# Cutting the last two rows of a row-sum kernel into other pieces: row 7 in five instead of four, row 6 in two instead of three

## The chip, the cores and the metric

One core of one Trainium2 chip. The time is the device time of one execution, in microseconds (us). DVE is VectorE, ACT is ScalarE, SP the engine that issues most transfers (SPq in the profile).

## The reference

```python
# x, y: float32, 1024 rows of 4096 columns; axis = -1
def reference(x, y, axis):
    return np.sum(np.abs(x - y), axis=axis).astype(np.float32)
```

33.55 MB are read, 4 KB are written, and each element needs a subtraction, an absolute value and an addition.

## The kernel before

Each of the 128 partitions holds eight rows, called row 0 to row 7 here. Rows 0 to 3 of x and of y are loaded by one transfer each. Then x rows 4 to 6 follow in one transfer, and their y rows one by one, each as soon as a buffer of y is free. Row 7 comes in pieces, x and y of each piece by a transfer of their own. DVE subtracts; ACT takes the absolute value and sums along the row in the same instruction, and a read of its accumulator (186 to 188 ns in the profile of before) follows each. The last piece of row 7 doesn't go through ACT. DVE writes its difference beside the sums that ACT left of the other pieces and closes with one reduction over both, with absolute values.

```python
PIECES = [1984, 1088, 640, 384]      # row 7
ROW6 = [2048, 1024, 1024]            # row 6
# ... transfers of rows 0 to 6 cut
    o = 0
    for i, w in enumerate(PIECES):
        c = slice(o, o + w)
        put(lambda: nc.sync.dma_start(out=xb[:, H - 1, c], in_=xr[:, K - 1, c]).then_inc(s_piece[i], 16))
        if i == 0:
            put(lambda: nc.sync.wait_ge(s_sub, H))
        put(lambda: nc.sync.dma_start(out=yb[:, H - 1, c], in_=yr[:, K - 1, c]).then_inc(s_piece[i], 16))
        o += w

    def sub(tx, ty, waits):          # DVE
        for s, v in waits:
            put(lambda: nc.vector.wait_ge(s, v))
        put(lambda: nc.vector.tensor_sub(out=tx, in0=tx, in1=ty).then_inc(s_sub, 1))
        count[0] += 1

    def absum(tx, to, sem):          # ACT
        put(lambda: nc.scalar.wait_ge(s_sub, count[0]))
        put(lambda: nc.scalar.activation(tx, tx, ABS, accum_out=to).then_inc(sem, 1))
        count[1] += sem is s_act
# ... rows 0 to 3 cut
    for k in range(H - 2):           # rows 4 and 5, whole
        sub(xb[:, k, :], yb[:, k, :], ([(s_xb, 16)] if k == 0 else []) + [(s_row[k], 16)])
        absum(xb[:, k, :], ro[:, H + k:H + k + 1], s_act)
    o = 0
    for i, w in enumerate(ROW6):     # row 6
        c = slice(o, o + w)
        sub(xb[:, H - 2, c], yb[:, H - 2, c], [(s_row[H - 2], 16)] if i == 0 else [])
        absum(xb[:, H - 2, c], part6[:, i:i + 1], s_act)
        o += w
    done6 = count[1]
    o = 0
    for i, w in enumerate(PIECES):   # row 7
        c = slice(o, o + w)
        tx, ty = xb[:, H - 1, c], yb[:, H - 1, c]
        if i == 1:                   # the sums of row 6's parts
            put(lambda: nc.vector.wait_ge(s_act, done6))
            put(lambda: nc.vector.reduce_sum(out=ro[:, K - 2:K - 1], in_=part6, axis=AX).then_inc(s_end, 1))
        if i < n_part:
            sub(tx, ty, [(s_piece[i], 32)])
            absum(tx, last[:, i:i + 1], s_end)
        else:
            put(lambda: nc.vector.wait_ge(s_piece[i], 32))
            put(lambda: nc.vector.tensor_sub(out=last[:, n_part:n_part + w], in0=tx, in1=ty).then_inc(s_end, 1))
            put(lambda: nc.vector.wait_ge(s_end, n_part + 2))
            put(lambda: nc.vector.reduce_sum(out=ro[:, K - 1:K], in_=last, axis=AX, apply_absolute_value=True).then_inc(s_end, 1))
        o += w
# ... store of ro cut
```

## Time and profile before

| | before |
|---|---|
| median of 3 runs (range) | 86.20 us (85.93 to 86.25) |
| span of the profiled run | 84.3 us |
| subtraction of row 5 starts | 65.58 us |
| row 5 starts on ACT | 70.04 us |
| last landing seen by DVE (0.02 us before its subtraction starts at 80.66) | 80.64 us |
| closing reduction | 81.41 to 81.97 us |

The last rows of the table are read from the timelines. Such a line gives start, length, engine, line of the program, operation, what it writes and reads, shape and count; in brackets stands how long the engine had been idle before it and what ended that. Two lines of the kernel before that the prediction leans on without showing them, from the timeline of all engines: the last issue of a load on SP, and row 5 on ACT.

```profile
61.71 2.67 SPq L96 DMA_DIRECT2D yb_rows<-in_y_dram  x1
...
70.04 3.62 ACT L110 ACTIVATE xb_rows<-xb_rows 128x4096 f32<-128x4096 f32 x1 [1.11 <-DVE xb_rows L105]
```

The second is the last ACT line with a bracket: for 1.11 us ACT had nothing to do until DVE was through with row 5.

### The profile page before, as it was taken

What the parts mean: (1) busy time and instruction counts of PE and PEld (TensorE: products, weight loads), DVE (VectorE), ACT (ScalarE), POOL (GpSimd) and SP (SyncE); (2) the same over time, 40 slices, a digit from 0 to 9 for tenths busy, and PEclk for the clock granted to TensorE, in tenths of its full rate; (3) what the DMA queues carried; (4) which work ended last, traced back from release to release, by engine and by line L of the source; (5) the groups of instructions that cost most, each with busy time, mean ns of one, the idle gap of its engine ahead of it and who ended that gap; (6) DMA issues with size and microseconds to landing.
All of it is one profiled execution on the core that took longest, in us unless ns stands there. A gap on an engine that the chain in (4) does not pass through costs nothing.

```text
span 84.3 us, 98 instructions
## 1 busy us (share of the span) xinstructions
DVE 36.5 (43%) x15; ACT 31.2 (37%) x25; POOL 0.2 (0%) x4
## 2 busy tenths in 40 slices
DVE  0000000000000000000399999999199897988870
ACT  5000000000000000000002979797970967999950
POOL 0000000000000000000000000000000000000000
DMA  9199999983999999749999888899999999999900
GB/s 497 62 435 497 497 497 497 497 373 155 466 497 497 497 497 497 342 187 466 396 606 490 373 373 373 381 427 427 420 443 412 451 404 414 425 397 404 341 0 2
DMA packets 2160, 33.56 MB, mean 398 GB/s; under 512 B 368, under 2 KB 624, under 8 KB 1392
## 3 DMA queue, kind: packets, MB, share of 16 engines
q1 hardware_dynamic: 2016, 25.17, 70.9%
q10 hardware_dynamic: 144, 8.39, 23.0%
HBM read 33.55 MB, written 0.00 MB: 398 GB/s over the span
## 4 chain that ended last, share of the span: by engine, by line
DMA 67%; DVE 16%; ACT 13%; ACTq 1%; issue 0%
DMA yb_rows<-in_y_dram 67%; ACT xb_rows L110 13%; DVE xa_rows L105 10%; DVE xb_rows L105 5%; ACTq L176 1%; DVE ro_sums L140 1%
## 5 line engine op out<-in xcount | busy, mean ns | idle before, releaser
L105 DVE TENSOR_TENSOR xa_rows<-xa_rows,yb_rows 128x4096 f32<-128x4096 f32 x4 | 17.4, 4421 | 41.5 <-DMA yb_rows<-in_y_dram 41.5
L110 ACT ACTIVATE xa_rows<-xa_rows 128x4096 f32<-128x4096 f32 x4 | 14.5, 3617 | 45.6 <-DVE xa_rows L105 45.6
L105 DVE TENSOR_TENSOR xb_rows<-xb_rows,yb_rows 128x4096 f32<-128x4096 f32 (+5 forms) x8 | 17.8, 2241 | 3.5 <-DMA yb_rows<-in_y_dram 3.4
L110 ACT ACTIVATE xb_rows<-xb_rows 128x4096 f32<-128x4096 f32 (+5 forms) x8 | 14.9, 1859 | 3.7 <-DVE xb_rows L105 3.7
L110 ACT ACT_TABLE_LOAD x1 | 1.3, 1283 | 0.9 <-PEq L162 0.9
L110 ACT ACTIVATION_READ_ACCUMULATOR xb_rows<-xb_rows 128x1 f32 x8 | 1.5, 188 | 0.0
L110 ACT ACTIVATION_READ_ACCUMULATOR xa_rows<-xa_rows 128x1 f32 x4 | 0.7, 186 | 0.0
L140 DVE TENSOR_REDUCE ro_sums<-last_piece 128x1 f32<-128x387 f32 x1 | 0.6, 556 | 0.2 <-ACT xb_rows L110 0.2
L138 DVE TENSOR_TENSOR last_piece<-xb_rows,yb_rows 128x384 f32<-128x384 f32 x1 | 0.6, 557 | 0.2 <-DMA yb_rows<-in_y_dram 0.2
L132 DVE TENSOR_REDUCE ro_sums<-part_sums 128x1 f32<-128x3 f32 x1 | 0.2, 156 | 0.2 <-ACT xb_rows L110 0.2
L162 POOL MEMSET const-bfloat16-1.0<- 128x1 bf16 x1 | 0.1, 102 | 0.0
L162 POOL MEMSET const-uint8-127<- 128x1 uint8 x1 | 0.1, 102 | 0.0
L162 POOL MEMSET const-float32-0.0<- 128x1 f32 x1 | 0.1, 99 | 0.2 <-issue 0.2
L162 POOL MEMSET const-float32-1.0<- 128x1 f32 x1 | 0.1, 99 | 0.0
## 6 DMA issues: line engine op xcount, KB each, us to landing
xb_rows<-in_x_dram SPq DMA_DIRECT2D x1, 6144.0 KB, 54.9
yb_rows<-in_y_dram SPq DMA_DIRECT2D x3, 2048.0 KB, 15.3
xb_rows<-in_x_dram SPq DMA_DIRECT2D x1, 992.0 KB, 17.9
yb_rows<-in_y_dram SPq DMA_DIRECT2D x1, 992.0 KB, 16.4
xb_rows<-in_x_dram SPq DMA_DIRECT2D x1, 544.0 KB, 17.4
yb_rows<-in_y_dram SPq DMA_DIRECT2D x1, 544.0 KB, 18.2
xb_rows<-in_x_dram SPq DMA_DIRECT2D x1, 320.0 KB, 18.6
yb_rows<-in_y_dram SPq DMA_DIRECT2D x1, 320.0 KB, 18.9
```

Of the source, the lines that this page charges most:

```text
L105: put(lambda: nc.vector.tensor_sub(out=tx, in0=tx, in1=ty).then_inc(s_sub, 1))
L110: put(lambda: nc.scalar.activation(tx, tx, ABS, accum_out=to).then_inc(sem, 1))
L132: put(lambda: nc.vector.reduce_sum(out=ro[:, K - 2:K - 1], in_=part6, axis=AX).then_inc(s_end, 1))
L138: put(lambda: nc.vector.tensor_sub(out=last[:, n_part:n_part + w], in0=tx, in1=ty).then_inc(s_end, 1))
L140: put(lambda: nc.vector.reduce_sum(out=ro[:, K - 1:K], in_=last, axis=AX, apply_absolute_value=True).then_inc(s_end, 1))
L162: nc = _bacc.Bacc("TRN2", target_bir_lowering=False, num_devices=1)
L176: with _tile.TileContext(nc) as tc:
```

## The change

The intent that can be read from it: a smaller last piece leaves less to subtract and to reduce behind the last landing, and a row 6 in two parts saves an instruction. The whole diff:

```diff
-PIECES = [1984, 1088, 640, 384]
-ROW6 = [2048, 1024, 1024]
+PIECES = [1920, 928, 640, 352, 256]
+ROW6 = [2304, 1792]
@@
-        if i == 1:
+        if i == 2:
             put(lambda: nc.vector.wait_ge(s_act, done6))
             put(lambda: nc.vector.reduce_sum(out=ro[:, K - 2:K - 1], in_=part6, axis=AX).then_inc(s_end, 1))
```

## The prediction

> **What bounds the kernel now.** I read the page's head and slices first, then the chain that ended last, then the timeline of the last fifteen microseconds engine by engine, and last the DMA table. The page:
>
> ```profile
> span 84.3 us, 98 instructions
> DVE 36.5 (43%) x15; ACT 31.2 (37%) x25; POOL 0.2 (0%) x4
> DMA  9199999983999999749999888899999999999900
> q1 hardware_dynamic: 2016, 25.17, 70.9%
> q10 hardware_dynamic: 144, 8.39, 23.0%
> ```
>
> No engine is busy for half the span, while the DMA row is near full until the last two slices and the two queues together take 93.9% of the engines' time. 33.55 MB have to come in; the kernel is DMA-bound until the last bytes have landed, and only the tail behind them is open to this change. The chain of work in order of time shows how that tail hangs on the rest:
>
> ```profile
> 50.24 15.32 DMA yb_rows<-in_y_dram
> 65.58 4.44 DVE xb_rows L105
> 70.04 10.61 ACT xb_rows L110 x12
> 81.28 0.10 ACT xb_rows L110
> 81.41 0.56 DVE ro_sums L140
> ```
>
> The end does not follow from the last transfer. It follows from row 5 (landed at about 65.56 us), its subtraction, and then ACT, which from 70.04 us on is never idle. The timelines of the two engines, ACT first and then DVE:
>
> ```profile
> 73.66 1.90 ACT L110 ACTIVATE xb_rows<-xb_rows 128x2048 f32<-128x2048 f32 x1
> 77.62 1.84 ACT L110 ACTIVATE xb_rows<-xb_rows 128x1984 f32<-128x1984 f32 x1
> 79.47 1.10 ACT L110 ACTIVATE xb_rows<-xb_rows 128x1088 f32<-128x1088 f32 x1
> 80.56 0.72 ACT L110 ACTIVATE xb_rows<-xb_rows 128x640 f32<-128x640 f32 x1
> 81.19 0.19 ACT L110 ACTIVATION_READ_ACCUMULATOR xb_rows<-xb_rows 128x1 f32 x1
> ...
> 75.30 2.23 DVE L105 TENSOR_TENSOR xb_rows<-xb_rows,yb_rows 128x1984 f32<-128x1984 f32 x1 [0.26 <-DMA yb_rows<-in_y_dram]
> 79.68 0.83 DVE L105 TENSOR_TENSOR xb_rows<-xb_rows,yb_rows 128x640 f32<-128x640 f32 x1 [0.36 <-DMA yb_rows<-in_y_dram]
> 80.66 0.56 DVE L138 TENSOR_TENSOR last_piece<-xb_rows,yb_rows 128x384 f32<-128x384 f32 x1 [0.15 <-DMA yb_rows<-in_y_dram]
> 81.41 0.56 DVE L140 TENSOR_REDUCE ro_sums<-last_piece 128x1 f32<-128x387 f32 x1 [0.19 <-ACT xb_rows L110]
> ```
>
> The reader is to see two runners. DVE waits for each piece to land (75.28, 79.66, 80.64 us) and has the last difference ready at 80.66 + 0.56 = 81.22. ACT has no bracket of idle time on any of these lines and is through at 81.19 + 0.19 = 81.38. The closing reduction waits for the later of the two, so ACT sets its start, with DVE 0.16 us ahead of it.
>
> [...] Here each ACTIVATE is followed by a 188 ns read of the accumulator that overlaps both neighbours, so I take the cost of one from start to start: from 70.04 to 80.56 there are six with 11264 columns, 10.52 us[...]. [...] a whole y row (16 KB per partition) came in 4.90 us (65.56 to 70.46, 428 GB/s), piece 0 (7.9 KB) in 4.82 us (421 GB/s), pieces 1 and 2 together in 4.38 us (404 GB/s), piece 3 (1.5 KB) in 0.98 us (401 GB/s).
>
> **The change, part by part.** It moves nothing before row 6: row 5 lands, is subtracted and starts on ACT at 70.04 as now.
>
> *Row 6 in two.* ACT has one instruction fewer: minus 0.189 us. DVE's first part [...] is ready at 70.48 + 2.56 = 73.04, before ACT is free at 73.66. The second starts about 0.08 us before that end (as neighbours on DVE overlap now: 70.48 + 2.29 = 72.77, next start 72.69), takes 2.02 and is ready at 74.98. ACT: 73.66 + 2.11 (2304) = 75.77, + 1.68 (1792) = 77.45, against 77.62 now.
>
> *Row 7 in five.* ACT takes all but the last piece: 1920+928+640+352 = 3840 columns in four instructions, against 3712 in three. [...] With row 6 the instructions cancel, seven before and seven after from 70.04 on. The net for ACT is **+0.107 us**.
>
> This holds only if ACT is still fed in time. Landing times, at the 2.54 us per 1000 columns of row 7 that 4.38 us for 1728 columns give, counted from 1984 columns at 75.28: 1920 at 75.12, 2848 at 77.47, 3488 at 79.09, 3840 at 79.99, 4096 at 80.64. Differences ready[...]: piece 0 at 77.30, piece 1 at 78.61, piece 2 at 79.93, piece 3 at 80.53, piece 4 at 81.08. ACT wants them at 77.45, 79.24, 80.20 and 80.93. Each is there, by 0.15, 0.63, 0.27 and 0.40 us. ACT stays unbroken, and its last one (352 columns; 640 take 0.82 us from start to the end of the read, so 0.58) ends at 81.50, against 81.38.
>
> *Reduction of row 6 one piece later.* It takes 0.16 us and now stands after piece 1, so DVE does it at about 78.6 while it would wait for piece 2 (79.09). Before it sat in a gap as well (77.75 to 77.91, piece 1 landing by my rate at 78.04). Worth nothing either way.
>
> *Last piece 256 instead of 384.* DVE's last difference is done at 81.08 instead of 81.22, but it is not what the end waits for. The closing reduction reads 4+256 = 260 elements instead of 387. From 556 ns at 387 and 156 ns at 3 the slope is 1.04 ns per element, so it takes 424 ns: **minus 0.132 us**, and this is on the path.
>
> *Two more transfers.* 2 x 144 = 288 more packets (the 144 of queue q10 are one transfer), 18 more per DMA engine. From the rates above, piece 0 lost 4.82 - 4.74 = about 0.08 us against a whole row's rate over 18 packets per engine, so I put the last landing 0.1 us later at most: DVE ready at 81.18, still 0.3 us ahead of ACT. Hidden.
>
> *Sum.* +0.107 - 0.132 = -0.025 us. The reduction starts at about 81.52 and ends at 81.94 against 81.97; the store behind it is unchanged. The bound moves not at all; DVE only waits longer for ACT.
>
> **The rivals.**
> (a) *The last landing and what follows it set the end.* Then smaller last pieces pay: 0.13 us in the subtraction, 0.13 in the reduction, 0.19 in the wait, together some 0.4 us, about 85.8 us. For it speaks that DMA is full to 80.6; against it the 0.19 us that the reduction waits for ACT today, and ACT without a gap since 70.04.
> (b) *A new wait breaks ACT's run.* Piece 0 is ready just 0.15 us before ACT wants it, piece 2 only 0.27 us. If landings slip by 0.3 us, ACT loses 0.1 to 0.2 us and the time is 86.3 to 86.4.
> (c) *The extra transfers hold up the queue.* The last issue of a y piece took 2.67 us on SP (61.71 to 64.38) where the others took 0.33 to 0.46, and two more come behind it. [...] the pieces landed 16 to 19 us after their issue. Even if the new issues wait for row 6 to land at 70.46, they are nearly 10 us early. I expect nothing of it.
>
> **Range and chances.** The runs before span 85.93 to 86.25 around 86.20. The change is a tenth of that scatter, so the prediction is 86.15 us. The range 85.75 to 86.50 covers rival (a) nearly in full at one end, (b) at the other, and the scatter. A 2% step is 1.72 us; the whole stretch from the last landing to the end of the reduction is 81.97 - 80.64 = 1.33 us, so no rearrangement of it can reach 2%. Faster 0.01, same 0.98, slower 0.01.
>
> **What would show it right or wrong.** Right: ACT's line in the chain again begins at 70.04 and runs unbroken, its last read-out ends 0.1 us later than now, the closing reduction takes 0.42 us and waits for ACT longer than today, some 0.4 us against 0.19. Wrong: idle time with a DVE releaser before one of ACT's last four activations (rival b); the closing reduction waiting for its own subtraction (rival a); a last landing later than 80.75 (packets dearer than I took them). A different start of row 5 would be scatter of the first 65 us of transfers, which the change does not touch and which could hide the whole effect.

Terms are cut from the prediction where the marks stand: what a column costs on ACT, how the 10.52 us split into columns and instructions, how long a subtraction of a given length takes on DVE, why smaller packets would come slower, and how a long issue is to be read. The sum was +0.107 us for 128 more columns on ACT, -0.189 us for the instruction that row 6 saves, +0.189 us for the one that row 7 adds, and -0.132 us for the reduction, together -0.025 us. What the traces give for the terms:

- *A column on ACT.* In the kernel before, ACTIVATEs of 4096 and 1024 columns took 3617 and 1042 ns, so 0.838 ns per column, and 128 columns come to 0.107 us.
- *An instruction on ACT.* pieces_only has one more than the changed kernel for the same columns. From row 5's start on ACT to the end of the last read it took 81.61 - 69.98 = 11.63 us against 81.63 - 70.19 = 11.44, so 0.19 us. The 0.189 was the estimate.
- *Row 6's parts.* In the changed kernel their subtractions took 2559 and 2018 ns, and on ACT they took 2.11 and 1.68 us from start to start, as the prediction has them.
- *Row 7's differences.* In the changed kernel they were ready at 77.46, 78.68, 79.94, 80.60 and 81.10 us; predicted, and moved by the 0.15 us by which row 5 came later there, 77.45, 78.76, 80.08, 80.68 and 81.23.

## The result

The changed kernel took 86.16 us (median of 6 runs, 86.11 to 86.27); the kernel before, beside it, 86.15 us (6 runs, 85.93 to 86.25). The ratio is 1.0008 with a 95% interval of 0.9993 to 1.0023: the same. The ratios and intervals here are those of the record, which takes them from the fast runs of both kernels; they are not quite the ratios of the medians.

The chain of work that ended last, changed kernel (start, length, what):

```profile
65.73 4.44 DVE xb_rows L105
...
70.19 10.87 ACT xb_rows L110 x11
...
81.15 0.49 ACT xb_rows L110 x2
81.63 0.02 issue
81.66 0.42 DVE ro_sums L140
```

It has the same form as before: row 5's subtraction, then ACT without a break, then the closing reduction. Row 5 came 0.15 us later than in the profiled run of before (65.73 against 65.58). Nothing of the change lies ahead of that point, and the profiled run is one of several that scatter by that much. So I compare the **tail**, from the start of row 5's subtraction to the end of the closing reduction: 81.97 - 65.58 = 16.39 us before, 82.08 - 65.73 = 16.35 us changed. The change saved 0.04 us in these two traces.

The timelines of ACT and then of DVE, changed kernel:

```profile
77.59 1.79 ACT L110 ACTIVATE xb_rows<-xb_rows 128x1920 f32<-128x1920 f32 x1
...
79.37 0.96 ACT L110 ACTIVATE xb_rows<-xb_rows 128x928 f32<-128x928 f32 x1
...
80.33 0.72 ACT L110 ACTIVATE xb_rows<-xb_rows 128x640 f32<-128x640 f32 x1
...
81.05 0.48 ACT L110 ACTIVATE xb_rows<-xb_rows 128x352 f32<-128x352 f32 x1
81.44 0.19 ACT L110 ACTIVATION_READ_ACCUMULATOR xb_rows<-xb_rows 128x1 f32 x1
...
79.11 1.49 DVE L105 TENSOR_TENSOR xb_rows<-xb_rows,yb_rows 128x640 f32<-128x640 f32 x2 [0.36 <-DMA yb_rows<-in_y_dram]
80.68 0.42 DVE L138 TENSOR_TENSOR last_piece<-xb_rows,yb_rows 128x256 f32<-128x256 f32 x1
81.66 0.42 DVE L140 TENSOR_REDUCE ro_sums<-last_piece 128x1 f32<-128x260 f32 x1 [0.55 <-ACT xb_rows L110]
```

The reader sees what the smaller last piece did. DVE has its last difference at 80.68 + 0.42 = 81.10, and then sits idle for 0.55 us, against 0.19 before, until ACT's last read at 81.63.

### The profile page after: what moved, and what is told of

The parts are those of the page before. It is cut to its first block, busy times and chain, and to the rows that moved or that the text cites. A ratio compares the mean times of both kernels' runs of the same rounds, so it can differ in the third digit from the quotient of the medians.

```text
span 84.5 us, 100 instructions
## 1 busy us (share of the span) xinstructions
DVE 36.3 (43%) x15; ACT 31.3 (37%) x25; POOL 0.2 (0%) x4
## 3 DMA queue, kind: packets, MB, share of 16 engines
q1 hardware_dynamic: 2304, 25.17, 70.7%
## 4 chain that ended last, share of the span: by engine, by line
DMA 67%; DVE 16%; ACT 13%; issue 0%; ACTq 0%
DMA yb_rows<-in_y_dram 67%; ACT xb_rows L110 13%; DVE xa_rows L105 10%; DVE xb_rows L105 5%; DVE ro_sums L140 1%; ACTq L176 0%
## 5 line engine op out<-in xcount | busy, mean ns | idle before, releaser
L110 ACT ACTIVATE xa_rows<-xa_rows 128x4096 f32<-128x4096 f32 x4 | 14.5, 3617 | 45.7 <-DVE xa_rows L105 45.7
L105 DVE TENSOR_TENSOR xb_rows<-xb_rows,yb_rows 128x4096 f32<-128x4096 f32 (+6 forms) x8 | 18.0, 2258 | 3.5 <-DMA yb_rows<-in_y_dram 3.3
L110 ACT ACTIVATE xb_rows<-xb_rows 128x4096 f32<-128x4096 f32 (+6 forms) x8 | 15.0, 1871 | 3.7 <-DVE xb_rows L105 3.7
```

## The experiments

All were correct against the reference. Each was timed in five rounds beside the kernel before on the same chip. The changed kernel's ratio in the table is the one given above. The tail is the sharper measure: it leaves out the scatter of the first 65 us. Each tail is from a single trace; changed, dve_plus and more_transfers, in which ACT has the same work, all give 16.35 us.

| kernel | row 5 subtraction starts | reduction ends | tail | ratio to before (95%) |
|---|---|---|---|---|
| before | 65.58 | 81.97 | 16.39 | |
| changed | 65.73 | 82.08 | 16.35 | 1.0008 (0.9993 to 1.0023) |
| pieces_only | 65.52 | 82.06 | 16.54 | 1.0009 (0.9996 to 1.0021) |
| row6_only | 65.69 | 82.09 | 16.40 | 1.0007 (0.9992 to 1.0023) |
| dve_plus | 65.57 | 81.92 | 16.35 | 1.0000 (0.9986 to 1.0015) |
| more_transfers | 65.53 | 81.88 | 16.35 | 0.9994 (0.9979 to 1.0009) |
| row5_split | 65.46 | 81.72 | 16.26 | 0.9985 (0.9972 to 0.9999) |
| split_old_pieces | 65.55 | 81.93 | 16.38 | 0.9991 (0.9976 to 1.0006) |
| freed5 | 65.58 | 81.63 | 16.05 | 0.9949 (0.9937 to 0.9961) |
| freed6 | 65.61 | 81.51 | 15.90 | 0.9941 (0.9927 to 0.9956) |

The theory: ACT, busy without a break from row 5 on, decides when the closing reduction starts. The main rival: the last landing and DVE's work behind it decide.

### Half of the change: the pieces alone (pieces_only)

Against the changed kernel:

```diff
-ROW6 = [2304, 1792]
+ROW6 = [2048, 1024, 1024]
```

> Row 7 in five pieces, row 6 left in three parts (2048, 1024, 1024). Theory (ACT's unbroken run from row 5 on sets the closing reduction): against the kernel before ACT has 128 more columns and one more instruction, +0.107 + 0.189 = +0.30 us, and the reduction is 0.13 us shorter, so +0.16 us from row 5's start on ACT to the end of the reduction (11.93 us before, so 12.09), no idle time on ACT. Rival (the last landing and what follows it set the end): 0.3 to 0.4 us less than before, about 11.55 us, whatever row 6 does.

Measured: from row 5's start on ACT to the end of the reduction 82.06 - 69.98 = 12.08 us. DVE's last two lines:

```profile
80.50 0.43 DVE L138 TENSOR_TENSOR last_piece<-xb_rows,yb_rows 128x256 f32<-128x256 f32 x1
81.64 0.42 DVE L140 TENSOR_REDUCE ro_sums<-last_piece 128x1 f32<-128x260 f32 x1 [0.71 <-ACT xb_rows L110]
```

The theory's 12.09 is met, the rival's 11.55 is off by half a microsecond, and ACT has no bracket of idle time behind row 5. The five pieces by themselves cost 0.15 us of tail; DVE waits 0.71 us for ACT.

### The other half: row 6 alone (row6_only)

```diff
-ROW6 = [2048, 1024, 1024]
+ROW6 = [2304, 1792]
```

This is the kernel before with that one line of the change.

> Row 7 in the four pieces of before, row 6 in two parts (2304, 1792). ACT's work from row 5 on is 0.19 us less than before. If ACT's work alone sets the end: -0.19 us. Theory with the feeding counted: piece 0 (1984) is subtracted only 7.5 us after row 5 starts on ACT, about 0.1 us after ACT is free, and piece 2 as well is ready only 0.03 us before ACT ended its run in the kernel before; so ACT gets a small gap and the gain shrinks to 0.01 to 0.05 us, 11.88 to 11.92 us from row 5's start on ACT to the end of the reduction. Rival (landing): 0 as well, but with the reduction waiting for the last subtraction and not for ACT.

Measured: 82.09 - 70.14 = 11.95 us, 0.02 more than before (11.93), where I had expected 0.01 to 0.05 less. So the size missed by a little, with the sign. The timelines of ACT and DVE show the mechanism:

```profile
77.45 0.19 ACT L110 ACTIVATION_READ_ACCUMULATOR xb_rows<-xb_rows 128x1 f32 x1
77.68 1.86 ACT L110 ACTIVATE xb_rows<-xb_rows 128x1984 f32<-128x1984 f32 x1
79.45 0.19 ACT L110 ACTIVATION_READ_ACCUMULATOR xb_rows<-xb_rows 128x1 f32 x1
79.54 1.09 ACT L110 ACTIVATE xb_rows<-xb_rows 128x1088 f32<-128x1088 f32 x1
80.54 0.18 ACT L110 ACTIVATION_READ_ACCUMULATOR xb_rows<-xb_rows 128x1 f32 x1
80.67 0.74 ACT L110 ACTIVATE xb_rows<-xb_rows 128x640 f32<-128x640 f32 x1
...
75.42 2.23 DVE L105 TENSOR_TENSOR xb_rows<-xb_rows,yb_rows 128x1984 f32<-128x1984 f32 x1 [0.34 <-DMA yb_rows<-in_y_dram]
79.82 0.82 DVE L105 TENSOR_TENSOR xb_rows<-xb_rows,yb_rows 128x640 f32<-128x640 f32 x1 [0.37 <-DMA yb_rows<-in_y_dram]
81.53 0.56 DVE L140 TENSOR_REDUCE ro_sums<-last_piece 128x1 f32<-128x387 f32 x1 [0.22 <-ACT xb_rows L110]
```

From start to start, an ACTIVATE follows the read in front of it by some 0.09 us when it is back to back (79.45 to 79.54). Before piece 0 it follows by 0.23 us (77.45 to 77.68), because piece 0 has been subtracted only at 75.42 + 2.23 = 77.65, and before piece 2 by 0.13 us, with the subtraction done at 80.64. The saved instruction (0.19 us) turned into waiting for pieces. The two ACTIVATEs that had waited were also 12 and 15 ns longer than the same shapes back to back in the kernel before (1856 against 1844, 736 against 721). The closing reduction still waits for ACT (0.22 us), where the rival had it waiting for the last subtraction. But the chain that ended last now goes back to the landing of piece 0 (75.40 us) and no longer to row 5. Row 6 in two parts alone is worth nothing. In the changed kernel it pays, since it takes off 0.19 of the 0.29 us that the five pieces put on ACT (from row 5's start there to the end of the last read 11.34 us before, 11.63 in pieces_only, 11.44 changed): 16.54 falls to 16.35.

### Work in DVE's slack (dve_plus)

Against the changed kernel:

```diff
+    idle = sbuf("idle_tile", [P, 224])
@@
             put(lambda: nc.vector.tensor_sub(out=last[:, n_part:n_part + w], in0=tx, in1=ty).then_inc(s_end, 1))
+            put(lambda: nc.vector.tensor_sub(out=idle, in0=yb[:, 0, 0:224], in1=yb[:, 0, 224:448]))
             put(lambda: nc.vector.wait_ge(s_end, n_part + 2))
```

> The changed kernel with one more subtraction on DVE (224 columns into a tile that nobody reads[...]), set between the last difference and the closing reduction, where DVE sat idle for 0.55 us in the changed kernel. Theory (ACT sets the closing reduction): no change, 16.35 us from the start of row 5's subtraction to the end of the reduction, and the idle time before the reduction falls from 0.55 to about 0.2 us. Rival (the last landing and DVE's work behind it set the end): 0.3 to 0.39 us more.

DVE's timeline in the tail:

```profile
80.56 0.42 DVE L139 TENSOR_TENSOR last_piece<-xb_rows,yb_rows 128x256 f32<-128x256 f32 x1
80.91 0.38 DVE L140 TENSOR_TENSOR idle_tile<-yb_rows 128x224 f32<-128x224 f32 x1
81.50 0.42 DVE L142 TENSOR_REDUCE ro_sums<-last_piece 128x1 f32<-128x260 f32 x1 [0.21 <-ACT xb_rows L111]
```

The tail is 16.35 us as in the changed kernel, and the wait for ACT fell from 0.55 to 0.21 us, both as expected. 0.38 us of useless work directly ahead of the last reduction (the rival's upper figure counts it as 0.39) costs nothing. This refutes the rival for the changed kernel.

### More transfers (more_transfers)

```diff
-        put(lambda: nc.sync.dma_start(out=xb[:, H - 1, c], in_=xr[:, K - 1, c]).then_inc(s_piece[i], 16))
-        if i == 0:
-            put(lambda: nc.sync.wait_ge(s_sub, H))
-        put(lambda: nc.sync.dma_start(out=yb[:, H - 1, c], in_=yr[:, K - 1, c]).then_inc(s_piece[i], 16))
+        halves = [c] if i < 3 else [slice(o, o + w // 2), slice(o + w // 2, o + w)]
+        for h in halves:
+            # the same two transfers and wait, with h for c
# ... waits for pieces 3 and 4: 64 instead of 32
```

> The changed kernel with each transfer of its last two pieces cut into two halves: four transfers more, 576 packets, same computation. Theory: packets of 0.5 to 0.7 KB cost a little, the last landing comes 0 to 0.2 us later (14.93 us after the start of row 5's subtraction in the changed kernel), and the end does not move, for DVE has 0.55 us in hand: 16.35 us. Rival (issues hold up the queue: the last two issues of the changed kernel already took 3.6 and 2.0 us): the four more issues wait for pieces to land, the last ones come after 75 us, the last landing slips by over 0.5 us and the end with it.

Three of the issues on SP, the last one among them, and the last two lines of DVE:

```profile
64.39 3.57 SPq L95 DMA_DIRECT2D xb_rows<-in_x_dram  x1
68.00 1.95 SPq L98 DMA_DIRECT2D yb_rows<-in_y_dram  x1
...
74.87 0.68 SPq L98 DMA_DIRECT2D yb_rows<-in_y_dram  x1
...
80.79 0.43 DVE L140 TENSOR_TENSOR last_piece<-xb_rows,yb_rows 128x256 f32<-128x256 f32 x1 [0.21 <-DMA yb_rows<-in_y_dram]
81.46 0.42 DVE L142 TENSOR_REDUCE ro_sums<-last_piece 128x1 f32<-128x260 f32 x1 [0.24 <-ACT xb_rows L112]
```

The issues are held up, until 75.55 us, yet the last difference starts only at 80.79 - 65.53 = 15.26 us after row 5's subtraction. That is 0.31 us later than in the changed kernel (80.68 - 65.73 = 14.95), more than the 0 to 0.2 that I had expected and less than the rival's 0.5. The reduction still waits 0.24 us for ACT, and the tail is 16.35 us: hidden behind ACT, as expected. Whether the 0.31 us come from the added packets or from the late issues no kernel here separates. Even with four more transfers the slip costs nothing at the end, because DVE has the room.

### ACT relieved, by starting row 5 sooner (row5_split, split_old_pieces)

ACT's unbroken run can start sooner if it needn't wait for all of row 5, so its 1.11 us of idle time ahead of row 5 is used. row5_split is the changed kernel with this:

```diff
+ROW5 = [2304, 1792]
-    for k in range(H - 2):
-        # rows 4 and 5, whole, then ROW6
+    sub(xb[:, 0, :], yb[:, 0, :], [(s_xb, 16), (s_row[0], 16)])
+    absum(xb[:, 0, :], ro[:, H:H + 1], s_act)
+    for j, row in enumerate([ROW5, ROW6]):
+        o = 0
+        for i, w in enumerate(row):
+            c = slice(o, o + w)
+            sub(xb[:, j + 1, c], yb[:, j + 1, c], [(s_row[j + 1], 16)] if i == 0 else [])
+            absum(xb[:, j + 1, c], part[:, j, i:i + 1], s_act)
+            o += w
# ... one reduction gives the sums of rows 5 and 6 from part
```

> The changed kernel, and row 5 also in two parts (2304, 1792), so that ACT starts row 5 at half of its subtraction, some 1.1 us sooner, for one more instruction (0.19 us). Its sums of rows 5 and 6 are reduced by one instruction. Theory: ACT is then 0.9 us ahead until piece 0, for which it waits, and has only its run behind piece 0: the gap that ACT leaves before piece 0 is about 0.5 us, and the end comes 0.11 us sooner than in the changed kernel. Counted from the landing of row 5 (the start of its subtraction) to the end of the reduction: 16.35 us in the changed kernel, so 16.24. If ACT's work before row 7 did not matter (rival: landing sets the end), nothing changes.

ACT's timeline of row 7:

```profile
77.22 1.80 ACT L112 ACTIVATE xb_rows<-xb_rows 128x1920 f32<-128x1920 f32 x1 [0.38 <-DVE xb_rows L107]
...
79.02 0.96 ACT L112 ACTIVATE xb_rows<-xb_rows 128x928 f32<-128x928 f32 x1
...
79.98 0.72 ACT L112 ACTIVATE xb_rows<-xb_rows 128x640 f32<-128x640 f32 x1
...
80.70 0.48 ACT L112 ACTIVATE xb_rows<-xb_rows 128x352 f32<-128x352 f32 x1
```

The tail is 16.26 us (expected 16.24). ACT now waits 0.38 us for piece 0, where about 0.5 was expected (another 0.34 us goes into a wait for row 6, which the expectation did not have), and is without a break only behind it. The bound has moved from row 5 to piece 0, and the end came 0.09 us sooner. split_old_pieces has the same rows 5 and 6, and row 7 in the pieces of before:

```diff
-PIECES = [1920, 928, 640, 352, 256]
+PIECES = [1984, 1088, 640, 384]
# ... the reduction of the sums again at i == 1
```

> Rows 5 and 6 in parts of 2304 and 1792 as in row5_split, but row 7 in the four pieces of the kernel before. With row5_split it makes, together with before and changed, a square of two factors. Theory: with ACT ahead, the old pieces end when the last but one (640) has gone through: landed, subtracted, 0.82 us on ACT; the end is 16.38 us after the start of row 5's subtraction, as before (16.39), so relief of ACT is worth nothing with the old pieces and 0.09 us with the new (16.26 measured in row5_split); the new pieces are worth 0.12 us with relief and 0.04 without. If relief of ACT alone did it: 16.28 here.

ACT at piece 0:

```profile
77.53 1.86 ACT L112 ACTIVATE xb_rows<-xb_rows 128x1984 f32<-128x1984 f32 x1 [0.60 <-DVE xb_rows L107]
```

The tail is 16.38 us as expected: there ACT waits 0.60 us for piece 0 and the end stays where it was. So in the kernel before, a second path, from the landings of row 7's pieces through their subtractions and ACT, was only some 0.01 us shorter than the one from row 5; with the old pieces, relief of ACT ahead of row 7 alone had nothing to win. The four kernels make a square, which is cleaner with row6_only (row 6 in two parts, like the other three) than with the kernel before:

| tail, us | four pieces | five pieces | worth of five pieces |
|---|---|---|---|
| row 5 whole | 16.40 (row6_only; kernel before, row 6 in three parts: 16.39) | 16.35 | 0.05 |
| row 5 in two parts | 16.38 | 16.26 | 0.12 |

The five pieces are worth more than twice as much once ACT has room ahead of them. These are differences of single traces; the two tails of the lower row were forecast to within 0.02 us before they ran.

### Pieces cut for both engines (freed5, freed6)

From the numbers of the first traces I estimated when each piece lands (2.54 us per 1000 columns), is subtracted and leaves ACT, and looked for the cut in which ACT and the last subtraction finish together. Against row5_split:

```diff
# freed5
-ROW6 = [2304, 1792]
-PIECES = [1920, 928, 640, 352, 256]
+ROW6 = [2048, 2048]
+PIECES = [1728, 1088, 608, 384, 288]
# freed6
+ROW6 = [2176, 1920]
+PIECES = [1600, 1056, 576, 384, 256, 224]
```

> Row 5 in two parts as in row5_split, row 6 in 2048 and 2048, row 7 in pieces of 1728, 1088, 608, 384, 288, which by the model of landings, subtractions and ACT let ACT and the last subtraction finish together. Theory: the reduction starts about 0.05 us after the last landing's subtraction, ACT waits shortly for nearly every piece of row 7, and from the start of row 5's subtraction to the end of the reduction it is 16.03 us, against 16.38 before and 16.35 changed: -0.33 us, some 0.4% of the time, ratio 0.996. If ACT were not what held the changed kernel, this would give at most the 0.03 us longer reduction, a loss.

> As freed5, with row 7 in six pieces of 1600, 1056, 576, 384, 256, 224 and row 6 in 2176 and 1920. Theory: from the start of row 5's subtraction to the end of the reduction 15.90 us (freed5 16.05, before 16.39), about -0.5 us on the kernel before, ratio 0.9935 to 0.995, if two more transfers cost nothing in the last landing; if a pair of transfers costs 0.1 us at the last landing, 16.0, no better than freed5.

freed5: tail 16.05 us (expected 16.03), 85.76 us (85.70 to 85.82) against 86.19 for the kernel before. freed6: tail 15.90 us (expected 15.90), 85.66 us (85.58 to 85.80) against 86.17. The two last lines of DVE in freed5:

```profile
80.61 0.46 DVE L140 TENSOR_TENSOR last_piece<-xb_rows,yb_rows 128x288 f32<-128x288 f32 x1 [0.18 <-DMA yb_rows<-in_y_dram]
81.17 0.46 DVE L142 TENSOR_REDUCE ro_sums<-last_piece 128x1 f32<-128x292 f32 x1
```

The last subtraction waits for its landing, and the reduction's line has no bracket any more: at the end neither engine waits long for the other. freed5's last piece (288) is larger than the changed kernel's (256), and yet its tail is 0.30 us shorter. So it is not the size of the last piece that makes the time here, but whether ACT is done with the others. Both freed5 and freed6 are clear of the kernel before (0.9949 and 0.9941), though by the 2% measure still the same. Neither was timed beside the changed kernel, whose own ratio is 1.0008. In freed6 the chain that ended last goes back through ACT to row 6 (landed at 70.48 us), so ACT still sets its end. Two more transfers than the changed kernel cost freed6 nothing visible at the landing: its last difference starts 80.59 - 65.61 = 14.98 us after row 5's subtraction.

## Why the prediction was right

The time (86.15 predicted, 86.16 measured) and the class hold; a change of 0.03 us can't be told from none by run times alone, and that the two agree to 0.01 us, where runs of one kernel scatter over 0.3 us, is luck. So the steps are judged by the traces.

- **ACT sets the end, and the path starts at row 5.** Shown, by dve_plus (0.38 us more work on DVE, the same tail of 16.35 us), by pieces_only (0.29 us more on ACT and 0.13 less in the reduction, a tail longer by 0.15) and by freed5. It held narrowly: split_old_pieces shows a path through the landings of row 7's pieces close behind it in the kernel before (16.38 against 16.39 us).
- **ACT's net of +0.107 us.** Predicted last read-out 11.46 us after row 5's start on ACT (81.50 - 70.04), measured 81.63 - 70.19 = 11.44, against 11.34 before: +0.10. The predicted starts of the four pieces of row 7, moved by the 0.15 us of scatter, are 77.60, 79.39, 80.35 and 81.08; measured were 77.59, 79.37, 80.33 and 81.05.
- **A reduction shorter by 0.132 us.** It took 424 ns instead of 556, as computed.
- **The sum, -0.025 us.** Measured -0.04 in the tail.
- **Rival (a), the landing and DVE's work behind it.** Refuted for the changed kernel: DVE was done 0.55 us before ACT, and 0.38 us more work on it cost nothing.
- **Rival (b), a new wait on ACT.** It didn't come in the changed kernel. row6_only shows how near it was: with the old piece 0 of 1984 columns the shorter row 6 ran into just that wait.
- **Rival (c), held-up issues.** The hold-up came. In the changed kernel too, the two issues behind the 2.71 us one took 3.57 and 1.95 us, the last until 70.15 us. It was harmless, as the prediction said (the last difference started 14.95 us after row 5's subtraction, 15.08 before), and stayed so for the end with four more.
- **One step was wrong, without effect.** The last landing was put up to 0.1 us later for the added packets (an estimate from the rates of before), hence a wait for ACT of 0.4 us. The last difference started 14.95 us after row 5's subtraction against 80.66 - 65.58 = 15.08 before, so 0.13 us sooner, and the wait became 0.55 us. The other kernels with a last piece of 256 and no further transfers give 14.98 or 14.99, those with one of 384 give 15.07 or 15.08. So it is not scatter of one trace. Piece 2 was early too: its subtraction starts at 79.11, so it landed at about 79.09, against 79.09 predicted and moved by 0.15 to 79.24. No transfer had been added up to there, so what was off includes the rate of landings (2.54 us per 1000 columns, carried over from the old pieces) and not only the 0.1 us put down for packets; its cause stays open.
- **A reading that was too smooth.** The prediction calls the DMA row near full until the last two slices. The row that it shows has slices of 1, 3, 7 and 4 tenths before 38 us. The change doesn't touch them, and the argument doesn't need them.

Not settled by experiment: how much of the 0.31 us in more_transfers comes from the added packets and how much from the late issues.

## What to carry to other kernels

When the last pieces of a stream are made smaller, look at which engine the closing step waits for: where another engine comes to it last, the gain can be lost there. Here the smaller pieces cost 0.29 us of instructions and columns on ACT (pieces_only) and won back 0.13 us in the closing step. Follow that engine back to its last idle time, and give it room there first; then cut the pieces so that both engines finish together. An instruction saved on a fully busy engine was worth its time here only where the next piece was already there: 0.19 us with the five pieces, nothing in row6_only.

## Lengths and times measured here

- The accumulator read behind an ACTIVATE took 186 to 188 ns on the mean (before, changed, row6_only, freed6) and overlapped both neighbours. From start to start such an ACTIVATE cost 0.72 us at 640 columns, 0.96 at 928, 2.11 at 2304 and 3.61 at 4096 (changed kernel).
- Three ACTIVATEs that had waited were longer than the same shape back to back: 1856 (row6_only) against 1844 ns (before) at 1984 columns, 736 (row6_only) against 721 ns (before) at 640, 1802 (freed6, row 6) against 1787 ns (changed) at 1920.
- A subtraction on DVE took 4421 ns at 4096 columns, 826 at 640 and 557 at 384 in the kernel before, 425 at 256 in the changed one and 394 at 224 in freed6.
- The closing reduction took 556 ns at 387 elements (before), 0.46 us at 292 (freed5), 424 ns at 260 (changed) and 391 at 229 (freed6). The reduction of row 6's three sums took 156 ns in the kernel before and 0.15 us in pieces_only.
- On SP, the first seven issues of row 7 took 0.33 to 0.46 us and the next three 2.71, 3.57 and 1.95 us in the changed kernel. Its last difference still started 14.95 us after row 5's subtraction, against 15.08 before.
- The last difference started 14.95 to 14.99 us after row 5's subtraction with a last piece of 256 columns (changed, pieces_only, dve_plus, row5_split) and 15.07 to 15.08 with one of 384 (before, row6_only, split_old_pieces), at the same total of bytes. Why is not shown.
